# Recurrent layer with both directions in one tile of 1024 columns, and two-operand work taken off GpSimd

## The chip, the cores and the metric

The kernel runs on one core of a Trainium2 chip. The metric is the device time of one execution, in microseconds (us). Engines are named as the profile names them: PE (TensorE matmul), PEld (its weight load), DVE (VectorE), ACT (ScalarE), POOL (GpSimd) and SP (SyncE, which issues the large DMAs). L1404 is line 1404 of the kernel before.

## The reference

The model has two residual layers over 512 tokens of width 1024. Each is a mixer followed by a squared-ReLU MLP of width 4096. Layer 0 mixes with a state-space scan and attention; layer 1, which the change is about, with a recurrent block (RG-LRU). Cut to layer 1's mixer:

```
gate, xr = split(u @ rec_w_in)                 # (512, 1024) each
xc = causal/centred width-4 depthwise conv of xr over tokens
for direction in (forward, backward):
    r = sigmoid(blockdiag(xc, ra_w[direction]) + ra_b[direction])
    i = sigmoid(blockdiag(xc, ix_w[direction]) + ix_b[direction])
    log_a = -8 * r * softplus(-lam[direction])
    a = exp(log_a)
    b = sqrt(-expm1(2 * log_a)) * (i * xc)
    h = scan over tokens of h[t] = a[t] * h[t-1] + b[t]   # reversed for backward
    hs.append(h)
y = (hs[0] + hs[1]) * gelu(gate)
h_res = h_res + g1 * (y @ rec_w_out)
```

Then `u = rms_norm(h_res) * (1 + scale) + shift` feeds `h_res + g2 * (square(relu(u @ w1)) @ w2)`.

## The kernel before

Activations lie with features on the 128 partitions and tokens on the 512 columns; a tensor of width 1024 is eight such tiles (k = 0 to 7). Matmuls reach float32 precision with three float32r products: every weight tile and every activation is split into a rounded part `hi` and a rest `lo`, and PE adds hi*hi, hi*lo and lo*hi (L555 to L557 for dense layers, L528 to L530 for the small gate matrices). Splitting a weight tile of 1024 columns takes a cast (L508 on ACT, or L506 on POOL) and a subtraction (L509, on DVE or POOL).

The program is built once. A scheduler sets each engine's order of instructions ahead of time, from its own estimate of durations; on the chip each engine then works through its list in that order, and waits on semaphores. At the norm boundaries, and in the first quarter of the recurrent input projection, PE's order is that of the source (`manual`).

The parts that matter here, in order of time:

- **Norm boundaries** (`boundary`, L843 to L845): the last output tiles of a layer are summed and normalized in two halves of 256 tokens, while PE already works on the first half of the next layer. Per tile DVE runs L843 and L845, ACT L844. The first four weight tiles of the next layer are split meanwhile, and three times, ahead of MLP 0, ahead of the recurrent layer and ahead of MLP 1, their `lo` is computed on POOL (`lo_eng`).
- **Recurrent layer** (`rglru`). The input projection is done in four quarters of 512 output features: two of the recurrent branch, then two of the gate branch. `fetch` copies the first into `xp`, in token order (L1333); `conv` runs one POOL instruction (L1339) and three DVE instructions (L1341); `parts` splits the result into `xh` and `xl`. `gates` does, for each k and direction d, two block-diagonal matmuls, two tanh (L1374, into `tr` and `ti`), an exp (L1377, `a`), a tanh (L1378, `th`), the square of `a` (L1379, on POOL or DVE) and two fused DVE instructions (L1380, L1381). This is done for k = 0 to 3 (group 0) and k = 4 to 7 (group 1). After each group, `roots` takes eight square roots (L1397), a product (L1401, POOL or DVE), the scan forward (L1404) and backward (L1407), and their sum (L1408, POOL). `branch` applies gelu to the gate branch, `merge` multiplies (L1423), and L1468 and L1469 split the result for the output projection, which ends in the next norm boundary.

Of the buffers, `tr` has two tiles, `a` and `ti` eight each, all of 512 columns. `tok` and `perm` are views of the same 512 tokens: contiguous, and with a step of four elements.

## Time and profile before

| what | value |
| --- | --- |
| median of 3 runs (lowest to highest) | 1296.41 us (1295.36 to 1296.78) |
| the profiled execution's own time | 1295.61 us |
| its span, first to last instruction | 1293.8 us |
| PE busy in the span | 1188.2 us (92%) |
| DVE busy | 847.5 us (66%) |
| ACT busy | 525.8 us (41%) |
| POOL busy | 350.2 us (27%) |
| mean granted PE clock | 0.959 |

Busy time is a share of the whole span; the stages have different limits, so the rows further down are cut by stretches of time. Times in them count from the span's start. The recurrent layer fills about 735 to 910 us. The mean duration of a group holds waiting too, where an instruction has started and can't go on; the least duration of a form, in the answers that print least/median/longest, is the one without it.

### The profile page before, as it was taken

How to read it: one execution, taken by the hardware profiler on the slowest of the kernel's cores; microseconds unless marked ns; L12 is line 12 of the kernel's file. 1: busy time of each engine (PE TensorE's matmuls, PEld its weight loads, DVE VectorE, ACT ScalarE, POOL GpSimd, SP SyncE). 2: the span in 40 equal slices, each digit the busy share in tenths (PEclk: the TensorE clock that was granted, in tenths of full speed). 3: DMA queues.
4: the chain of work that ended last, by engine and by line, in shares of the span. 5: the costliest groups of instructions: out<-in, count | busy, mean ns of one | idle time of the engine just before them, and what ended most of it. 6: DMA issues, size and time to landing. Idle time of an engine off the chain costs nothing.

```text
span 1293.8 us, 17211 instructions
## 1 busy us (share of the span) xinstructions
PE 1188.2 (92%) x6552; PEld 1006.7 (78%) x6552; DVE 847.5 (66%) x1234; ACT 525.8 (41%) x954; POOL 350.2 (27%) x394
## 2 busy tenths in 40 slices
PE   2689999899999999999999997769899999999997
PEld 2578677777988888888889875558898888888887
DVE  7458999977878866487334799897655332435243
ACT  3157557454443421243322357563444311334130
POOL 9896886500200000000002477571300000000000
PEclk9989789999999999999999998789899999999998
DMA  9321311065448766576222321103233233332311
GB/s 326 126 62 57 91 30 33 20 201 171 163 130 273 248 211 193 167 250 193 96 96 81 115 82 35 63 17 114 66 98 98 98 98 98 98 98 94 97 38 66
DMA packets 83859, 151.77 MB, mean 117 GB/s; under 512 B 5696, under 2 KB 30272, under 8 KB 83776
## 3 DMA queue, kind: packets, MB, share of 16 engines
q1 hardware_dynamic: 75712, 137.04, 32.5%
q10 hardware_dynamic: 8064, 13.64, 3.3%
q8 instruction: 51, 0.84, 0.3%
q14 instruction: 32, 0.26, 0.1%
HBM read 148.55 MB, written 2.10 MB: 116 GB/s over the span
## 4 chain that ended last, share of the span: by engine, by line
PE 59%; DVE 22%; POOL 9%; issue 5%; DMA 3%; ACT 2%; DVEq 0%; POOLq 0%; ACTq 0%
PE ps L555 10%; PE ps L556 10%; PE ps L557 10%; PE px L555 7%; PE px L556 7%; PE px L557 7%; DVE actb L447 3%; DVE actb L845 2%; DMA wr<-ada_w 1%; DMA wr<-w 1%; DVE wl L509 1%; PE po L983 1%; DVE th L1404 1%; POOL tiny L77 1%; DVE acc L637 1%
## 5 line engine op out<-in xcount | busy, mean ns | idle before, releaser
L509 DVE TENSOR_TENSOR wl<-wr,wh 128x1024 fp32r<-128x1024 f32 (+2 forms) x163 | 198.8, 1222 | 278.7 <-ACT wh L508 272.3
L508 ACT CAST wh<-wr 128x1024 fp32r<-128x1024 f32 (+2 forms) x170 | 173.2, 1021 | 428.3 <-PE ps L556 190.5
L556 PE MATMUL ps<-actb,wh 128*128 128x512 f32 (+1 forms) x512 | 183.8, 359 | 0.0
L509 POOL TENSOR_TENSOR wl<-wr,wh 128x1024 fp32r<-128x1024 f32 (+1 forms) x15 | 34.6, 2310 | 461.3 <-ACT wh L508 458.5
L555 PE MATMUL ps<-acta,wh 128*128 128x512 f32 (+1 forms) x328 | 119.0, 363 | 2.1 <-ACT xp L1333 1.6
L557 PE MATMUL ps<-acta,wl 128*128 128x512 f32 (+1 forms) x328 | 117.9, 360 | 0.0
L555 PE MATMUL ps<-hid,wh 128*128 128x512 f32 x288 | 112.1, 389 | 0.0
L557 PE MATMUL ps<-hid,wl 128*128 128x512 f32 x288 | 112.0, 389 | 0.0
L556 PE MATMUL ps<-hid,wh 128*128 128x512 f32 x288 | 112.0, 389 | 0.0
L556 PEld LDWEIGHTS ps<-actb,wh 128*128 128x128 f32 x512 | 99.7, 195 | 13.5
L555 PE MATMUL px<-hid,wh 128*128 128x512 f32 (+1 forms) x288 | 98.9, 343 | 0.0
L557 PE MATMUL px<-hid,wl 128*128 128x512 f32 (+1 forms) x288 | 98.5, 342 | 0.0
L556 PE MATMUL px<-hid,wh 128*128 128x512 f32 (+1 forms) x288 | 98.5, 342 | 0.0
L556 PE MATMUL px<-actb,wh 128*128 128x512 f32 (+1 forms) x224 | 85.5, 382 | 0.0
L637 DVE SCALAR_TENSOR_TENSOR acc<-wr,cact,acc 128x1024 f32<-128x1024 f32 x49 | 62.8, 1281 | 17.5 <-DMA wr<-ada_w 16.8
L555 PEld LDWEIGHTS ps<-acta,wh 128*128 128x128 f32 x328 | 64.3, 196 | 12.1 <-ACT xp L1333 2.0
L557 PEld LDWEIGHTS ps<-acta,wl 128*128 128x128 f32 x328 | 64.0, 195 | 8.9
L555 PE MATMUL ps<-actc,wh 128*128 128x512 f32 (+1 forms) x184 | 65.8, 358 | 0.0
L557 PE MATMUL ps<-actc,wl 128*128 128x512 f32 (+1 forms) x184 | 65.3, 355 | 0.0
L555 PEld LDWEIGHTS ps<-hid,wh 128*128 128x128 f32 x288 | 54.1, 188 | 11.2
L557 PEld LDWEIGHTS ps<-hid,wl 128*128 128x128 f32 x288 | 54.1, 188 | 11.2
L556 PEld LDWEIGHTS ps<-hid,wh 128*128 128x128 f32 x288 | 54.1, 188 | 11.2
(493 smaller groups left out, 2877.8 us busy)
## 6 DMA issues: line engine op xcount, KB each, us to landing
wr<-w SPq DMA_DIRECT2D x128, 512.0 KB, 3.7
wr<-ada_w SPq DMA_DIRECT2D x56, 512.0 KB, 4.3
wr<-wout SPq DMA_DIRECT2D x16, 512.0 KB, 3.4
...
```

Source lines behind the costliest of these rows:

```text
L77: self.eng.tensor_scalar(t, a, s, None, op0=op0)
L447: self.scan = V.tensor_tensor_scan(vv, m4, vv, 0.0, op0=ALU.mult, op1=ALU.add)
L508: nc.scalar.copy(hi, src)
L509: (lo_eng or nc.vector).tensor_tensor(lo, src, hi.bitcast(F32), op=ALU.subtract)
L555: mm(out, wh, xh, start=first and a == a0 and lead(o), stop=False, skip_group_check=True)
L556: mm(out, wh, xl, start=False, stop=False, skip_group_check=True)
L557: mm(out, wl, xh, start=False, stop=last and a == a0 + kk - 1, skip_group_check=True)
L637: nc.vector.scalar_tensor_tensor(acc, raw, self.ca[:, k:k + 1], acc, op0=ALU.mult, op1=ALU.add)
L845: nc.vector.scalar_tensor_tensor(lo, t, sh[:, k:k + 1], hi.bitcast(F32), op0=ALU.add, op1=ALU.subtract)
L983: self.nc.tensor.matmul(po[h2 * 64:h2 * 64 + 64, t * 128:(t + 1) * 128], self.vp[:, kb, v], pts[:, kb * 128:(kb + 1) * 128], start=(kb == ...
L1404: V.tensor_tensor_scan(hs, a, ti, 0.0, op0=ALU.mult, op1=ALU.add)
```

## The change

It moves work between engines and joins the two directions. It leaves the matmuls, the number of weight tiles and all DMAs as they are.

- `gates` works on tiles of 1024 columns, d = 0 in the left half and d = 1 in the right. The matmuls, tanh and exp stay at 512 columns. The square of `a` becomes one ACT instruction of 1024 columns, and L1380 and L1381 become one DVE instruction each of 1024 columns. `tr` has two tiles of 1024, `a`, `ti` and `th` four each.
- `roots` takes one square root (ACT) and one product (DVE) of 1024 columns for each k; the scans stay at 512; the sum of the directions goes to DVE, into a new tile `hs`.
- `merge` writes the product contiguously into the gate tile and splits it at once; the separate loop with L1468 and L1469, which read with a step of four, is dropped.
- The `lo` of the gate matrices (`gwl`) and the `lo` of the first four weight tiles at the three boundaries go from POOL to DVE.
- Left on POOL from the first MLP on: two memsets for each `xp`, the first step of `conv`, the `hi` casts of the gate matrices, of `xh` for k under 4 and of eight weight tiles. All have one tensor operand.
- The pool `sp` no longer rounds its small tiles up to 512 bytes, which with a pad frees 4 KB a partition.

```diff
--- before.py
+++ after.py
@@ -56,7 +56,7 @@
 NCONST = 772
 
 LINE = 128
-ROUNDED = ("sp", "hyb", "att", "s5", "out", "mlp")
+ROUNDED = ("hyb", "att", "s5", "out", "mlp")
 
 XP = 640
 
@@ -144,6 +144,7 @@
         self.ap = self.pool(ctx, "ap")
         self.sp = self.pool(ctx, "sp")
         self.tl(self.pool(ctx, "edge", side="right"), "pad", [P, 120])
+        self.tl(self.sp, "pad", [P, 56])
         ct = self.cp.tile([P, NCOL], F32, tag="cols", name="cols_sb")
         nc.sync.dma_start(ct, cols)
         kt = self.cp.tile([P, NCONST], F32, tag="consts", name="consts_sb")
@@ -1276,12 +1277,12 @@
                 del hid[:]
                 for g in range(4):
                     if c == 0 and g == 0:
-                        self.hold, self.lo_eng = self.wdma, nc.gpsimd
+                        self.hold = self.wdma
                         with self.manual():
                             for hf, outs in enumerate(self.lin_half(w1, u, 0, 4, fresh=True)):
                                 for o in range(4):
                                     hidden(o, slice(hf * 256, hf * 256 + 256), outs[o])
-                                self.hold = self.lo_eng = None
+                                self.hold = None
                         continue
                     ps = self.lin(w1, u, c * 2048 + g * 512)
                     if side:
@@ -1346,7 +1347,7 @@
                     A.copy(hi, src)
                 else:
                     G.tensor_scalar(hi, src, 1.0, 0.0, op0=ALU.mult, op1=ALU.add)
-                (G if scalar is None else V).tensor_tensor(lo, src, hi.bitcast(F32), op=ALU.subtract)
+                V.tensor_tensor(lo, src, hi.bitcast(F32), op=ALU.subtract)
 
             def gate_split(k):
                 hi = self.tl(rp, "gwh", [P, 512], F32R, bufs=2)
@@ -1359,28 +1360,30 @@
                 split2(xh, xl, xc, k >= 4)
                 return xc, xh, xl
 
+            both = lambda t: t.rearrange("p (d n) -> p d n", d=2)
+
             def gates(k, xc, xh, xl):
 
-                out = []
                 wh, wl = gws[k] if k < 2 else gate_split(k)
+                tr = self.tl(rp, "tr", [P, 1024], bufs=2)
+                ti = self.tl(rp, "ti", [P, 1024], bufs=4)
                 for d in range(2):
                     j = d * 8 + k
-                    tr = self.tl(rp, "tr", [P, 512], bufs=2)
-                    ti = self.tl(rp, "ti", [P, 512], bufs=8)
                     for kind, o, b in ((0, tr, hra), (1, ti, hix)):
                         g = slice((d * 2 + kind) * P, (d * 2 + kind + 1) * P)
                         ps = self.psum("pn" if (d, kind) == (0, 1) else "px")
                         self.mm3(ps, wh[:, g], wl[:, g], xh, xl, True, True)
-                        sig = A.activation(o, ps, AF.Tanh, bias=b[:, j:j + 1], scale=0.5)
-                    a = self.tl(rp, "a", [P, 512], bufs=8)
-                    th = self.tl(rp, f"th{d}", [P, 512], bufs=8 - 4 * d)
-                    A.activation(a, tr, AF.Exp, bias=nsp4[:, j:j + 1], scale=nsp4[:, j:j + 1])
-                    last = A.activation(th, tr, AF.Tanh, bias=sp4[:, j:j + 1], scale=sp4[:, j:j + 1])
-                    (V if k < 4 and d == 1 else G).tensor_tensor(tr, a, a, op=ALU.mult)
-                    V.scalar_tensor_tensor(th, tr, 1.0, th, op0=ALU.add, op1=ALU.mult)
-                    V.scalar_tensor_tensor(ti, ti, 1.0, xc, op0=ALU.add, op1=ALU.mult)
-                    out.append((a, th, ti))
-                return out, (sig, last)
+                        sig = A.activation(both(o)[:, d], ps, AF.Tanh, bias=b[:, j:j + 1], scale=0.5)
+                a = self.tl(rp, "a", [P, 1024], bufs=4)
+                th = self.tl(rp, "th", [P, 1024], bufs=4)
+                for d in range(2):
+                    j = d * 8 + k
+                    A.activation(both(a)[:, d], both(tr)[:, d], AF.Exp, bias=nsp4[:, j:j + 1], scale=nsp4[:, j:j + 1])
+                    A.activation(both(th)[:, d], both(tr)[:, d], AF.Tanh, bias=sp4[:, j:j + 1], scale=sp4[:, j:j + 1])
+                last = A.activation(tr, a, AF.Square)
+                V.scalar_tensor_tensor(th, tr, 1.0, th, op0=ALU.add, op1=ALU.mult)
+                V.scalar_tensor_tensor(both(ti), both(ti), 1.0, xc.unsqueeze(1).to_broadcast([P, 2, 512]), op0=ALU.add, op1=ALU.mult)
+                return (a, th, ti), (sig, last)
 
             def behind(ins):
                 st = ExitStack()
@@ -1391,21 +1394,16 @@
             def roots(g, gt, after):
 
                 with behind(after):
-                    for o in range(4):
-                        for d in range(2):
-                            th = gt[o][d][1]
-                            last = (A.activation(th, th, AF.Sqrt, scale=0.25),)
-                for o in range(4):
-                    for d in range(2):
-                        a, th, ti = gt[o][d]
-                        (V if g == 0 and d == 1 else G).tensor_tensor(ti, ti, th, op=ALU.mult)
-                        if d == 0:
-                            hs = th
-                            V.tensor_tensor_scan(hs, a, ti, 0.0, op0=ALU.mult, op1=ALU.add)
-                            hfs[g * 4 + o] = hs
-                        else:
-                            V.tensor_tensor_scan(ti[:, ::-1], a[:, ::-1], ti[:, ::-1], 0.0, op0=ALU.mult, op1=ALU.add)
-                            G.tensor_tensor(hs, hs, ti, op=ALU.add)
+                    for a, th, ti in gt:
+                        last = (A.activation(th, th, AF.Sqrt, scale=0.25),)
+                for o, (a, th, ti) in enumerate(gt):
+                    V.tensor_tensor(ti, ti, th, op=ALU.mult)
+                    hs = self.tl(rp, "hs", [P, 512], bufs=8)
+                    a, ti = both(a), both(ti)
+                    V.tensor_tensor_scan(hs, a[:, 0], ti[:, 0], 0.0, op0=ALU.mult, op1=ALU.add)
+                    V.tensor_tensor_scan(ti[:, 1, ::-1], a[:, 1, ::-1], ti[:, 1, ::-1], 0.0, op0=ALU.mult, op1=ALU.add)
+                    V.tensor_tensor(hs, hs, ti[:, 1], op=ALU.add)
+                    hfs[g * 4 + o] = hs
                 return last
 
             def branch(ps, after, gg=()):
@@ -1418,17 +1416,24 @@
                 return gg, last
 
             def merge(g, gg):
+
                 for o in range(4):
-                    hs = hfs[g * 4 + o]
-                    V.tensor_tensor(perm(hs), tok(gg[o]), perm(hs), op=ALU.mult)
-
+                    if o % 2 == 0:
+                        hi2, lo2 = (both(self.tl(rp, t, [P, 1024], F32R, bufs=4)) for t in ("a", "ti"))
+                    hi, lo = hi2[:, o % 2], lo2[:, o % 2]
+                    V.tensor_tensor(tok(gg[o]), tok(gg[o]), perm(hfs[g * 4 + o]), op=ALU.mult)
+                    A.copy(hi, gg[o])
+                    V.tensor_tensor(lo, gg[o], hi.bitcast(F32), op=ALU.subtract)
+                    ys.append((hi, lo))
+
+            ys = []
             xps = [None] * 4
-            self.hi_eng, self.lo_eng = None, G
+            self.hi_eng = None
             with self.manual():
                 for hf, outs in enumerate(self.lin_half(win, u, 1024, 4, fresh=True)):
                     for o in range(4):
                         xps[o] = fetch(o, outs[o], hf, xps[o])
-            self.hi_eng, self.lo_eng = G, None
+            self.hi_eng = G
             last = ()
             cvs = [None] * 4
             for g in range(2):
@@ -1461,13 +1466,6 @@
             merge(0, gg)
             gg, last = branch(ps, last)
             merge(1, gg)
-            ys = []
-            for o in range(8):
-                hi = self.tl(rp, "a", [P, 512], F32R, bufs=8)
-                lo = self.tl(rp, "ti", [P, 512], F32R, bufs=8)
-                A.copy(tok(hi), perm(hfs[o]))
-                V.tensor_tensor(tok(lo), perm(hfs[o]), tok(hi).bitcast(F32), op=ALU.subtract)
-                ys.append((hi, lo))
             self.rotate(["ps", "ps", "ps", "ps", "px", "px", "px"])
 
             def upd(k, sl, ps):
```

The order of the instructions moves at these places. The first is DVE's list at the norm boundary ahead of the recurrent layer, from the second half of the first 256 tokens to the statistics of the other half. Before (L845 writes the `lo` half of the new activations, L1272 updates the residual, L730 and L733 are the statistics):

```order
L845 SCALAR_TENSOR_TENSOR actb_6783<-nt_6784,mod_4813,acta_6782 128x256
L845 SCALAR_TENSOR_TENSOR actb_6789<-nt_6784,mod_4813,acta_6788 128x256
L1272 SCALAR_TENSOR_TENSOR h_3732<-px_6690,mod_4422,h_3732 128x256
L1272 SCALAR_TENSOR_TENSOR h_3736<-px_6690,mod_4422,h_3736 128x256
L845 SCALAR_TENSOR_TENSOR actb_6794<-nt_6795,mod_4813,acta_6793 128x256
L845 SCALAR_TENSOR_TENSOR actb_6800<-nt_6795,mod_4813,acta_6799 128x256
L730 TENSOR_SCALAR nr1x_6921<-pn_6914 128x2
```

Of the change, the same stretch (its line numbers are one higher from L147 on):

```order
L1273 SCALAR_TENSOR_TENSOR h_3733<-px_6691,mod_4423,h_3733 128x256
L1273 SCALAR_TENSOR_TENSOR h_3737<-px_6691,mod_4423,h_3737 128x256
L510 TENSOR_TENSOR wl_7008<-wr_7006,wh_7007 128x1024
L846 SCALAR_TENSOR_TENSOR actb_6784<-nt_6785,mod_4814,acta_6783 128x256
L846 SCALAR_TENSOR_TENSOR actb_6790<-nt_6785,mod_4814,acta_6789 128x256
L846 SCALAR_TENSOR_TENSOR actb_6795<-nt_6796,mod_4814,acta_6794 128x256
L1350 TENSOR_TENSOR gwl_7169<-gw_6862,gwh_7168 128x512
L846 SCALAR_TENSOR_TENSOR actb_6801<-nt_6796,mod_4814,acta_6800 128x256
L1350 TENSOR_TENSOR gwl_7182<-gw_6864,gwh_7181 128x512
L731 TENSOR_SCALAR nr1x_6922<-pn_6915 128x2
```

Four `wl` (three of them earlier in the list) and two `gwl` now stand in DVE's own list between the norm's instructions, where POOL ran them beside it.

The second place is DVE's list at the end of group 1, from the last fused instruction to the first `lo` of the output projection's activations (scans are printed as SCALAR_TENSOR_TENSOR). Before:

```order
L1380 SCALAR_TENSOR_TENSOR th_1611_7860<-tr_7847,th_1611_7860 128x512
L1404 SCALAR_TENSOR_TENSOR th_1546_7603<-a_7602,ti_7591 128x512
L1407 SCALAR_TENSOR_TENSOR ti_7610<-a_7621,ti_7610 128x512
L1404 SCALAR_TENSOR_TENSOR th_1567_7686<-a_7685,ti_7674 128x512
L1423 TENSOR_TENSOR th_1456_7227<-xh_7866,th_1456_7227 128x4x128
L1423 TENSOR_TENSOR th_1475_7306<-xl_7867,th_1475_7306 128x4x128
L1407 SCALAR_TENSOR_TENSOR ti_7693<-a_7704,ti_7693 128x512
L1423 TENSOR_TENSOR th_1496_7389<-xh_7868,th_1496_7389 128x4x128
L1423 TENSOR_TENSOR th_1514_7463<-xl_7869,th_1514_7463 128x4x128
L1404 SCALAR_TENSOR_TENSOR th_1588_7769<-a_7768,ti_7757 128x512
L509 TENSOR_TENSOR wl_8084<-wr_8082,wh_8083 128x1024
L1469 TENSOR_TENSOR ti_8047<-th_1456_7227,a_8046 128x512
```

Of the change (L1400 is the product of 1024 columns, L1403 and L1404 the scans, L1405 the sum, L1424 the merge, L1426 the `lo`):

```order
L1384 SCALAR_TENSOR_TENSOR th_7799<-tr_7776,th_7799 128x1024
L1400 TENSOR_TENSOR ti_7560<-ti_7560,th_7582 128x1024
L1403 SCALAR_TENSOR_TENSOR hs_7944<-a_7581,ti_7560 128x512
L1404 SCALAR_TENSOR_TENSOR ti_7560<-a_7581,ti_7560 128x512
L1400 TENSOR_TENSOR ti_7777<-ti_7777,th_7799 128x1024
L1424 TENSOR_TENSOR xh_7807<-xh_7807,hs_7484 128x512
L1405 TENSOR_TENSOR hs_7944<-hs_7944,ti_7560 128x512
L1424 TENSOR_TENSOR xl_7810<-xl_7810,hs_7499 128x512
L510 TENSOR_TENSOR wl_8013<-wr_8011,wh_8012 128x1024
L510 TENSOR_TENSOR wl_8043<-wr_8041,wh_8042 128x1024
L1404 SCALAR_TENSOR_TENSOR ti_7777<-a_7798,ti_7777 128x512
L1426 TENSOR_TENSOR ti_7968<-xh_7807,a_7967 128x512
```

Rows of the same kind are left out of both: from the last fused instruction to the first `lo` DVE's list of the change holds four products, eight scans, four merges, two sums and two `wl`. The products and sums are new on DVE here.

The third place is PE's list for the gates of k = 5 to 7 (L529 to L531 of the change are the gate matmuls, L556 to L558 the dense ones). Before, at most twelve gate matmuls stood in a row. Of the change, the end of a run of 30:

```order
L529 MATMUL px_7778<-xh_7673,gwh_7772 128x512
L529 MATMUL px_7788<-xh_7673,gwh_7772 128x512
L529 MATMUL px_7793<-xh_7673,gwh_7772 128x512
L529 MATMUL pn_7783<-xh_7673,gwh_7772 128x512
L530 MATMUL px_7778<-xl_7674,gwh_7772 128x512
L531 MATMUL px_7778<-xh_7673,gwl_7773 128x512
L531 MATMUL px_7793<-xh_7673,gwl_7773 128x512
L556 MATMUL ps_7815<-acta_6761,wh_7820 128x512
```

The dense matmuls of the third quarter stand ahead of that run and the 96 of the last quarter behind it, where before the two kinds alternated and 69 dense ones were left behind the last gate. SP's list of DMAs is the same in both.

## Rows read from the trace of the kernel before

**Rows 1.** The page's busy times: us, share of the span, instructions.
```profile
PE 1188.2 (92%) x6552; PEld 1006.7 (78%) x6552; DVE 847.5 (66%) x1234; ACT 525.8 (41%) x954; POOL 350.2 (27%) x394
```

**Rows 2.** Busy time by engine: first, second stretch, tail, output projection; a ten-us one.
```profile
735.00:788.20 53.20, 48.48 (x221) 38.80 (x220) 48.32 (x47) 28.95 (x42) 39.53 (x37) 0.98 0.30 96
788.20:844.80 56.60, 42.29 (x143) 31.63 (x142) 50.27 (x48) 35.84 (x51) 34.63 (x21) 0.75 0.11 38
844.80:870.20 25.40, 13.91 (x63) 11.19 (x61) 24.22 (x15) 17.72 (x25) 23.94 (x11) 0.81 0.03 7
870.20:910.50 40.30, 39.04 (x223) 34.41 (x223) 28.67 (x36) 13.78 (x21) 6.25 (x1) 0.95 0.31 101
...
840.00:850.00 10.00, 10.00 (x46) 8.29 (x45) 6.39 (x7) 9.54 (x15) 6.72 (x5) 1.00 0.01 2
```

**Rows 3.** What PE waited for, 735 to 890: us in total, times, longest.
```profile
PE ps L556 <- DVE ti L1469: 12.8, 2, 11.5
PE px L528 <- ACT tr L1374: 9.8, 4, 5.4
PE px L529 <- DVE xl L1349: 4.1, 3, 2.3
PE ps L555 <- ACT xp L1333: 1.6, 1, 1.6
```

**Rows 4.** DVE's forms by line: duration in ns least/median/longest, first and last start.
```profile
L1381 DVE SCALAR_TENSOR_TENSOR ti<-ti,xc x12: 677/900/1751, 756.4 to 834.0; 128x512 f32<-128x512 f32 x12
L1341 DVE SCALAR_TENSOR_TENSOR xc<-xp,cols_sb,xc x18: 739/1092/1527, 739.4 to 791.0; 128x512 f32<-128x512 f32 x18
L1404 DVE TENSOR_TENSOR_SCAN th<-a,ti x8: 1191/2264/2303, 798.5 to 871.0; 128x512 f32<-128x512 f32 x8
L1469 DVE TENSOR_TENSOR ti<-th,a x8: 1046/1072/2041, 868.1 to 888.0; 128x512 fp32r<-128x512 f32 x8
L1423 DVE TENSOR_TENSOR th<-xp,th x4: 1081/1098/1100, 873.2 to 883.9; 128x512 f32<-128x512 f32 x4
L509 DVE TENSOR_TENSOR wl<-wr,wh x20: 1193/1224/2276, 731.7 to 896.3; 128x1024 fp32r<-128x1024 f32 x20
```

**Rows 5.** POOL and DVE side by side: start, us, engine, line.
```profile
756.43 1.10 DVE L1381 SCALAR_TENSOR_TENSOR ti<-ti,xc 128x512 f32<-128x512 f32 x1
...
756.96 1.05 POOL L1348 TENSOR_SCALAR xh<-xc 128x512 fp32r<-128x512 f32 x1
757.97 1.29 POOL L1349 TENSOR_TENSOR gwl<-gw,gwh 128x512 fp32r<-128x512 f32 x1
...
758.04 1.77 DVE L1349 TENSOR_TENSOR xl<-xc,xh 128x512 fp32r<-128x512 f32 x1 [0.52 <-POOL xh L1348]
```

**Rows 6.** POOL's groups, 335 to 935: busy us, mean ns, idle before.
```profile
L509 POOL TENSOR_TENSOR wl<-wr,wh 128x1024 fp32r<-128x1024 f32 x12 | 29.2, 2434 | 461.3 <-ACT wh L508 458.5 <-issue 2.8
L1401 POOL TENSOR_TENSOR ti<-ti,th 128x512 f32<-128x512 f32 x12 | 23.9, 2019 | 2.0 <-ACT th L1397 2.0
```

**Rows 7.** ACT's groups, 735 to 890: busy us, mean ns, idle before.
```profile
L1377 ACT ACTIVATE a<-tr,rgc 128x512 f32<-128x512 f32 x16 | 13.0, 815 | 0.2
L508 ACT CAST wh<-wr 128x1024 fp32r<-128x1024 f32 x11 | 11.5, 1043 | 3.3 <-issue 2.7 <-PE ps L556 0.6
L1374 ACT ACTIVATE tr<-px,rgc 128x512 f32<-128x512 f32 x16 | 10.9, 687 | 27.4 <-PE px L530 12.0 <-DVE th L1380 11.7 <-PE pn L530 3.4
```

**Rows 8.** Norm boundaries: PE's waits, DVE behind POOL, and a stretch at half clock.
```profile
PE pn L802 <- DVE nr1y L735: 2.3, 1, 2.3
...
PE pn L795 <- DVE nacc L781: 3.8, 1, 3.8
...
916.12 5.26 DVE L845 SCALAR_TENSOR_TENSOR actb<-nt,mod,acta 128x256 fp32r<-128x256 f32 x3
...
929.00:936.00 7.00, 7.00 (x35) 7.00 (x35) 0.94 (x6) 0.20 (x1) 0.00 (x0) 0.51 0.18 63
```

**Rows 9.** POOL's longest single instruction of the recurrent layer.
```profile
877.58 6.25 POOL L1408 TENSOR_TENSOR th<-th,ti 128x512 f32<-128x512 f32 x1 [8.27 <-DVE ti L1407]
```

## The prediction

> **What bounds the kernel now.** I began with the page's busy times [rows 1]: PE is busy 92% of the span, so time is to be had only where PE waits or runs slowly. The table by stretches shows where that is [rows 2]: in the recurrent layer. From 788.2 to 844.8 us PE is busy 42.3 of 56.6 us, at a mean granted clock of 0.75, for 143 matmuls. At full rate (2.4 GHz) 46 matmuls of 512 columns take 10 us, 0.217 us each [rows 2], so these are 31 us of work. The list of PE's waits names what it lacked [rows 3]: DVE's `lo` tiles (L1469, L1349), and ACT's tanh, which waits for `tr`, which DVE's L1380 has to free. ACT is not full (35.8 us of that stretch), DVE nearly is (50.3) [rows 2].
>
> Much of DVE's time there is not work. The scan takes 1.19 us at least and 2.26 at the median, the fused L1381 0.68 and 0.90, with 1.75 at the longest [rows 4]. The side-by-side rows show the reason: DVE's subtraction that starts 0.07 us behind a two-operand POOL instruction takes 1.77 us instead of 0.68, so it stood until POOL's 1.29 us were over; behind a one-operand one L1381 took 1.10, a loss of 0.42 [rows 5]. POOL is busy 39.5, 34.6 and 23.9 us in the first three stretches [rows 2], and its products mean 2.02 us [rows 6]: the two engines block each other.
>
> The Trainium skill, "SBUF — State Buffer", section "Who interferes with whom", says that a DVE instruction with two SBUF inputs contends with any GpSimd instruction that reads SBUF, and that the later one blocks until the other ends. By that rule the change's line between one operand and two is none, and the time would be the 1305 us of the first rival below; the trace agrees that one-operand instructions block at all, with 0.42 us where POOL ran for 1.05 [rows 5].
>
> **The change, part by part.** Each price is a least duration [rows 4], since it counts work without blocking: 0.68 us for two inputs of 512 columns, 0.74 for a conv step, 1.2 for 1024 columns or a scan, 1.06 to 1.09 for a read with a step of four.
>
> DVE's work from 735 to 890 now: 17 weight `lo` x 1.2, 24 conv steps x 0.74, 52 instructions of 512 x 0.68, 16 scans x 1.2, 8 + 8 strided ones x 1.07 make 110 us. The change makes 32 fused ones of 512 into 16 of 1024 (21.8 to 19.2), the four products of 512 into eight of 1024 (2.7 to 9.6), drops four squares (2.7), adds six gate `lo` and eight sums (9.5), and takes the step out of eight `lo` (8.4 to 5.4): some 118 us. So DVE gets 8 us more work, and should get rid of the blocking behind two-operand instructions. POOL keeps 28 instructions of about 1.05 us [rows 5], 29 us instead of the 98 us of the first three stretches. Twelve weight `lo`, 29.2 us on POOL [rows 6], become 12 x 1.2 = 14.5 us on DVE, at the boundaries.
>
> *First stretch, 735 to 788.2 (group 0).* PE's waits on L1349 and on `xp`, up to 5.7 us [rows 3], are what can go; DVE's added and dropped work nearly cancel here. I take a **gain of 4**; the ends are 0 and 6.
>
> *Second stretch, 56.6 us: roots of group 0, gates of group 1.* DVE's list holds twelve instructions of 1024 (14.4), eight scans (9.6), eight sums and copies (5.4) and about eleven splits and conv steps (8.5): 38 us, plus a few us behind POOL. ACT has its 35.8 us now [rows 2] and four squares of 1024 columns; none stands in the trace, the nearest row is the cast of 1024 at 1.04 us [rows 7], so 40 us. Eight roots of 512 become four of 1024, counted even. PE needs 31. No engine needs more than 40, and the chain tanh, exp, square, fused product still runs through three engines; `tr`, with two tiles of 1024, now lets gates run a whole k ahead. I take 43 us, since DVE stands at most a k's work (some 3 us) in front of ACT: a **gain of 14**. The ends: 40, a gain of 17; or ACT's 40 with all the 20.8 us that it waits in this stretch today, a loss of 4.
>
> *Tail, 844.8 to 870.2.* PE's longest wait, 11.5 us, ends with the first L1469 [rows 3]. By its list DVE now runs four products, eight scans, four merges, two sums and two weight `lo` before that `lo`: 4.8 + 9.6 + 4.3 + 1.4 + 2.4 = 22.5 us, plus about 2 us until the first root of 1024 columns is out. That is about what the stretch took with blocking (25.4 less the `lo` itself): the moved products eat what the missing POOL gives. **Gain 0**, ends -3 and 3. PE meanwhile has 96 dense matmuls, 20.8 us.
>
> *Output projection, 870.2 to 910.5.* PE is busy 39.0 of 40.3 us at clock 0.95 [rows 2]: PE bounds it. The second wait on L1469, 12.8 less 11.5 us [rows 3], goes, and some of the slow clock: **gain 2**, ends 0 and 3.
>
> *The three boundaries.* PE waits 2.3 us ahead of the recurrent layer and 3.8 ahead of MLP 1, then runs 7 us at clock 0.51 (1.2 GHz for 2.4) [rows 8], 35 matmuls of half work lost, about 3.4 us; the clock fell behind the wait. DVE's L845, three of which took 5.26 us, stood behind POOL [rows 8]. Against that, DVE takes over four weight `lo`, 4.8 us, at each. The sums nearly balance, but at the first of these places the statistics no longer stand behind gate `lo` of POOL. **Gain 4** for all; the ends are 9 (waits and slow clock gone) and a loss of 7 (half of the 14.5 us uncovered).
>
> `sp`'s new packing I cost at nothing: no row prices it, and its tiles are written by instructions that lie beside PE's work. The memsets, table loads, DMAs and SP's order stay.
>
> The sum is 4 + 14 + 0 + 2 + 4 = **24 us**. From the profiled execution's 1295.61 us, of which 1293.8 are span, that leaves 1271.6; this execution lies 0.8 under the median of the runs, so I predict **1272 us**.
>
> **The rivals.**
>
> *One-operand POOL instructions block as much.* If each of the 28 costs DVE its 1.05 us, 29 us of blocking stay. What is there today is about 32 us: DVE's busy time to 890 (the first three stretches, 122.8 us, and some 19 of the 28.7 us behind them [rows 2]) less its 110 of work. Then DVE saves 3 and gets 8 more in the layer, and some 4 more at the boundaries: **1305 us**, slower than before. It decides at about 0.7 us per POOL instruction. (The rule of the Trainium skill's SBUF page, above, would give this.) For it: the one-operand instruction in the rows did cost 0.42 us. Against: 0.42 is well under 1.05, and a POOL list of 28 rarely meets DVE at the start of an instruction. Chance 10%, of which 2 in the band of no change.
>
> *POOL is starved instead.* With DVE's list dense in two-input instructions, POOL waits: L1408 took 6.25 us where DVE streamed [rows 9]. POOL still begins each conv and casts eight weight tiles. If each of eight k loses PE 1.5 us: 12 us, **1284 us**. Against: those steps are issued a k ahead. Chance 13%.
>
> *PE loses its filler.* PE's list now has 30 gate matmuls in a row ahead of the last quarter. They wait for ACT, which needs about 7 us per k (four tanh, four exp and tanh, a square [rows 7]) where PE needs 12 x 0.217 = 2.6. If PE's clock falls to half there, as it does today at mean 0.75 [rows 2], and half of the 96 dense matmuls behind the gates run at half clock, the tail waits for PE instead: about 10 us, **1282 us**. Chance 15%.
>
> *All of it.* The upper ends, 6 + 17 + 3 + 3 + 9 = 38 us: DVE's blocking was all that held PE. **1258 us**. Chance 12%.
>
> **How the numbers follow.** The forecast has 50%, between about 1264 and 1279. The range that takes in the three faster cases reaches from 1258 to 1287 and leaves out the slower rival and the outermost part of the ends. Faster than before by over 0.2% (2.6 us, about what a measurement of this kernel can tell from none): the forecast and the three cases, 90%. Within 0.2%: 3%. Slower: 7%.
>
> **What would show it.** Right: DVE's scans at 1.2 us at the median; DVE busier with fewer us per instruction; the second stretch near 43 us and the first `lo` of the output projection some 18 us earlier against the start of the layer; PE's mean clock there over 0.85; the wait of 2.3 us gone. Wrong: fused instructions of 1024 that take 1.6 us or more beside POOL's one-operand ones; PE waiting for weight tiles (`wh` of L506) or for `xh`; PE at half clock after 850 us; `wl` on DVE delaying L845 at the boundaries, so that the waits of 3.8 us grow.

## The result, and the profile after

The changed kernel takes **1261.7 us** (median of 4 runs, 1260.99 to 1262.24), the kernel before beside it 1296.6. The ratio is 0.973, with a 95% interval of 0.9713 to 0.9747: a gain of 33 to 37 us. The forecast was 1272, with a range of 1258 to 1287. The direction and the range held; the gain was under-sized by some 10 us.

The page's busy times of the changed kernel, to be read beside [rows 1]:

```profile
PE 1174.1 (93%) x6552; PEld 997.9 (79%) x6552; DVE 820.2 (65%) x1246; ACT 527.5 (42%) x954; POOL 244.9 (19%) x342
```

DVE runs twelve instructions more than before and is busy 27 us less, though by the forecast's prices it took over some 22 us of work. What went is time it had spent standing.

The table by stretches of the changed kernel, cut at the same events as [rows 2]: the first stretch, from the same matmul on, to the first roots; the second, to the last L1384; the tail, to PE's first matmul on a `lo` of the output projection; the output projection, to the first matmul of the next boundary's statistics; and the first 5.9 us of that projection alone. Columns: the window and its length, then busy us (instructions) of PE, PEld, DVE, ACT and POOL, the granted clock, DMA share, GB/s.

```profile
729.50:777.10 47.60, 47.60 (x228) 40.13 (x227) 42.85 (x44) 33.55 (x49) 26.60 (x29) 1.00 0.32 101
777.10:818.10 41.00, 32.26 (x117) 24.70 (x117) 38.19 (x42) 35.91 (x48) 3.31 (x3) 0.83 0.17 58
818.10:842.10 24.00, 18.70 (x82) 14.87 (x81) 22.85 (x23) 16.73 (x22) 0.00 (x0) 0.98 0.12 38
842.10:881.10 39.00, 39.00 (x221) 34.60 (x221) 23.84 (x35) 11.65 (x21) 0.00 (x0) 0.93 0.27 86
...
842.10:848.00 5.90, 5.90 (x14) 4.64 (x15) 5.90 (x8) 0.62 (x1) 0.00 (x0) 0.51 0.33 116
```

The first stretch takes 47.6 us (53.2 before), the second 41.0 (56.6), the tail 24.0 (25.4), the output projection 39.0 (40.3). POOL has nothing to do in the tail now. In the second stretch DVE (38.2 of 41.0) and ACT (35.9) are close to full and PE is not, so the bound has passed from blocking to work. The last row shows what a wait still costs: behind its wait of 4.4 us PE runs at a granted clock of 0.51, 1.2 GHz for 2.4.

PE's waits of the changed kernel, first from 730 to 890 us, then at the norm boundaries (us in total, times, longest). `nacc` and `nr1y` are steps of the norm's statistics. The rows answer to [rows 3] and [rows 8]:

```profile
PE ps L557 <- DVE ti L1426: 4.4, 1, 4.4
PE pn L529 <- ACT ti L1376: 4.2, 1, 4.2
PE px L530 <- DVE xl L1350: 2.8, 1, 2.8
PE px L529 <- ACT ti L1376: 1.5, 1, 1.5
...
PE pn L796 <- DVE nacc L782: 1.8, 1, 1.8
PE pn L803 <- DVE nr1y L736: 0.8, 1, 0.8
```

The wait for the first `lo` fell from 11.5 to 4.4 us. The 9.8 us of waits for tanh into `tr` are down to 0.2; waits for tanh into `ti`, 5.7 us, took part of their place. At the boundaries 5.9 us behind nacc (two waits, 2.1 and 3.8) became one of 1.8, and 2.3 became 0.8.

DVE's forms by line in the changed kernel (ns, least/median/longest), to be read against [rows 4]: the scans, the fused instruction of 1024 columns, conv and the weight `lo`:

```profile
L1403 DVE TENSOR_TENSOR_SCAN hs<-a,ti x8: 1211/1215/1228, 788.0 to 839.1; 128x512 f32<-128x512 f32 x8
L1385 DVE SCALAR_TENSOR_TENSOR ti<-ti,xc x6: 1212/1214/1214, 753.2 to 811.1; 128x1024 f32<-128x1024 f32 x6
L1342 DVE SCALAR_TENSOR_TENSOR xc<-xp,cols_sb,xc x18: 737/867/1528, 734.0 to 775.0; 128x512 f32<-128x512 f32 x18
L510 DVE TENSOR_TENSOR wl<-wr,wh x28: 1196/1222/1629, 698.4 to 894.0; 128x1024 fp32r<-128x1024 f32 x28
```

The forecast's price list holds to a few hundredths of a microsecond: the scan's median went from 2.26 us to 1.215. Of the forms shown, only the conv steps, which stand beside POOL's casts, still have a median well above their least.

### The profile page after: what moved, and what is told of

Its sections match the earlier page's. It is cut to its first block, busy times and chain, and to the rows that moved or that the text cites. A ratio compares the mean times of both kernels' runs of the same rounds, so it can differ in the third digit from the quotient of the medians.

```text
span 1260.4 us, 17174 instructions
## 1 busy us (share of the span) xinstructions
PE 1174.1 (93%) x6552; PEld 997.9 (79%) x6552; DVE 820.2 (65%) x1246; ACT 527.5 (42%) x954; POOL 244.9 (19%) x342
## 3 DMA queue, kind: packets, MB, share of 16 engines
q1 hardware_dynamic: 75712, 137.04, 33.4%
## 4 chain that ended last, share of the span: by engine, by line
PE 71%; DVE 15%; POOL 8%; issue 3%; ACT 3%; DMA 0%; DVEq 0%; ACTq 0%; POOLq 0%
PE ps L557 12%; PE ps L558 12%; PE ps L556 12%; PE px L556 8%; PE px L557 8%; PE px L558 8%; DVE actb L448 2%; DVE wl L510 2%; PE po L984 1%; POOL tiny L77 1%; DVE actb L443 1%; DVE s5m L442 1%; DVE actb L441 1%; DVE nb L966 1%; DVE ti L1404 1%
## 5 line engine op out<-in xcount | busy, mean ns | idle before, releaser
L510 DVE TENSOR_TENSOR wl<-wr,wh 128x1024 fp32r<-128x1024 f32 (+2 forms) x175 | 211.3, 1209 | 288.5 <-ACT wh L509 277.9
L557 PE MATMUL ps<-actb,wh 128*128 128x512 f32 (+1 forms) x512 | 181.1, 354 | 0.1
L556 PE MATMUL ps<-acta,wh 128*128 128x512 f32 (+1 forms) x328 | 116.5, 356 | 0.0
L558 PE MATMUL ps<-acta,wl 128*128 128x512 f32 (+1 forms) x328 | 115.9, 354 | 0.0
L556 PE MATMUL ps<-hid,wh 128*128 128x512 f32 x288 | 112.1, 389 | 0.0
L558 PE MATMUL ps<-hid,wl 128*128 128x512 f32 x288 | 112.0, 389 | 0.0
L556 PE MATMUL px<-hid,wh 128*128 128x512 f32 (+1 forms) x288 | 98.9, 343 | 0.0
L558 PE MATMUL px<-hid,wl 128*128 128x512 f32 (+1 forms) x288 | 98.4, 342 | 0.0
L556 PEld LDWEIGHTS ps<-acta,wh 128*128 128x128 f32 x328 | 62.7, 191 | 8.5
L558 PEld LDWEIGHTS ps<-acta,wl 128*128 128x128 f32 x328 | 62.6, 191 | 8.4
L556 PE MATMUL ps<-actc,wh 128*128 128x512 f32 (+1 forms) x184 | 65.1, 354 | 0.0
L558 PE MATMUL ps<-actc,wl 128*128 128x512 f32 (+1 forms) x184 | 64.8, 352 | 0.0
L556 PEld LDWEIGHTS ps<-hid,wh 128*128 128x128 f32 x288 | 54.1, 188 | 11.3
L558 PEld LDWEIGHTS ps<-hid,wl 128*128 128x128 f32 x288 | 54.1, 188 | 11.2
```

What stands on the lines that cost most here:

```text
L510: (lo_eng or nc.vector).tensor_tensor(lo, src, hi.bitcast(F32), op=ALU.subtract)
L556: mm(out, wh, xh, start=first and a == a0 and lead(o), stop=False, skip_group_check=True)
L557: mm(out, wh, xl, start=False, stop=False, skip_group_check=True)
L558: mm(out, wl, xh, start=False, stop=last and a == a0 + kk - 1, skip_group_check=True)
```

## The experiments

Twelve runs. Times are medians; the ratio is to the kernel before in the same session, with its interval. In the sessions the kernel before had medians of 1296.0 to 1297.0 us, so a difference between runs of two sessions is uncertain by about 1 us more.

| run | what it is | us | ratio |
| --- | --- | --- | --- |
| e1 | before, boundary `lo` on DVE | 1286.6 | 0.9918 (0.9903 to 0.9932) |
| e2 | before, layer's two-operand work off POOL | 1281.4 | 0.9875 (0.9861 to 0.9890) |
| e3 | e1 and e2 together | 1270.1 | 0.9788 (0.9771 to 0.9804) |
| e4 | changed, layer's two-operand work back on POOL, but for the squares | 1281.5 | 0.9877 (0.9863 to 0.9892) |
| e5 | changed, POOL's casts with two operands | 1275.0 | 0.9836 (0.9820 to 0.9852) |
| e6 | changed, old merge | 1262.0 | 0.9735 (0.9720 to 0.9749) |
| e7 | changed, gelu and merge of group 0 first | 1255.5 | 0.9685 (0.9671 to 0.9700) |
| e8 | before, new packing of `sp` | 1296.9 | 1.0000 (0.9991 to 1.0009) |
| e9 | e3 with four `tr` of 512 columns | 1262.4 | 0.9741 (0.9725 to 0.9758) |
| e10 | e7, backward scan into `th` | 1261.0 | 0.9724 (0.9704 to 0.9744) |
| e11 | before, four `tr` of 512 columns | 1296.3 | 0.9992 (0.9982 to 1.0001) |
| e12 | e7, all `xh` casts on POOL | 1259.5 | 0.9712 (0.9698 to 0.9726) |

### e1: the boundaries alone

```diff
-                        self.hold, self.lo_eng = self.wdma, nc.gpsimd
+                        self.hold = self.wdma
...
-            self.hi_eng, self.lo_eng = None, G
+            self.hi_eng = None
```

> The kernel before, with nothing changed but the engine of the twelve `lo` of weight tiles at the three norm boundaries: DVE for POOL. Theory (POOL's two-operand instructions held DVE up, at the boundaries too, and that part of the gain is about 9 us): 1288 us, 1286 to 1290, the waits of 2.1, 2.3 and 3.8 us for nacc and nr1y smaller, and L845 at its least duration. Rival (DVE only trades 29.2 us on POOL for 14.5 us of its own): 1294 to 1300.

Measured: 1286.6 us, 10.4 less than before (9 to 13 by the interval). The boundary ahead of MLP 1 in this run, in the timeline of DVE (start, us, engine, line, and in brackets the idle time before it), and then PE's waits of the boundaries:

```profile
906.47 1.23 DVE L509 TENSOR_TENSOR wl<-wr,wh 128x1024 fp32r<-128x1024 f32 x1 [2.63 <-ACT wh L508]
...
911.38 1.22 DVE L509 TENSOR_TENSOR wl<-wr,wh 128x1024 fp32r<-128x1024 f32 x1
912.51 1.66 DVE L845 SCALAR_TENSOR_TENSOR actb<-nt,mod,acta 128x256 fp32r<-128x256 f32 x4
```

```profile
PE pn L795 <- DVE nacc L781: 1.8, 1, 1.8
PE pn L802 <- DVE nr1y L735: 1.7, 1, 1.7
```

Four L845 take 1.66 us where three took 5.26 [rows 8], and a `wl` takes 1.23 us on DVE where POOL took 2.43 [rows 6]. The first of the four stands in time in which DVE was idle; the other three (from 911.38, 914.88 and 919.16 us) stand in its list, 1.22 us each, 3.7 in all. In the kernel before, the four on POOL cost DVE 5.9 us at this boundary, counted above the least durations: 4.0 on the three L845 of [rows 8], 0.6 on a step of the statistics, and 1.3 on these two L845, which take 0.87 us without blocking:

```profile
925.96 2.17 DVE L845 SCALAR_TENSOR_TENSOR actb<-nt,mod,acta 128x256 fp32r<-128x256 f32 x2
```

The theory holds: the `wl` cost DVE less in its own list than they had cost it from POOL. Two details differ. PE's waits at the boundaries fell by 4.7 us (8.2 to 3.5), so they are not the whole of the gain. And ahead of the recurrent layer four L845 still take 4.42 us, beside gate `lo` that this run leaves on POOL.

### e2, e3 and e4: the layer's two-operand work, with and without the joining

e2 changes the kernel before as follows, and nothing else; e3 has this and e1's edit.

```diff
-                (G if scalar is None else V).tensor_tensor(lo, src, hi.bitcast(F32), op=ALU.subtract)
+                V.tensor_tensor(lo, src, hi.bitcast(F32), op=ALU.subtract)
...
-                    last = A.activation(th, tr, AF.Tanh, bias=sp4[:, j:j + 1], scale=sp4[:, j:j + 1])
-                    (V if k < 4 and d == 1 else G).tensor_tensor(tr, a, a, op=ALU.mult)
+                    A.activation(th, tr, AF.Tanh, bias=sp4[:, j:j + 1], scale=sp4[:, j:j + 1])
+                    last = A.activation(tr, a, AF.Square)
...
-                        (V if g == 0 and d == 1 else G).tensor_tensor(ti, ti, th, op=ALU.mult)
+                        V.tensor_tensor(ti, ti, th, op=ALU.mult)
...
-                            G.tensor_tensor(hs, hs, ti, op=ALU.add)
+                            V.tensor_tensor(hs, hs, ti, op=ALU.add)
```

> The kernel before, at 512 columns and with its old merge, the boundaries' `lo` left on POOL; only the two-operand work of the recurrent layer leaves POOL: the gate `lo`, the products and the sums go to DVE, the squares to ACT (16 of 512 columns). DVE gets about 15 us more of least durations (26 moved instructions less four squares, 0.68 each). Theory (blocking): most of the 24 us that the layer and its output projection gave, less the 7 us that 512 columns cost DVE where they are not hidden: 1276 us, 1272 to 1280. Rival (the joining of the directions, with its deeper tr and fewer instructions, is what gave the gain): 1290 us or more, since DVE was nearly full.

> Both edits of the two runs ahead of this one together: the kernel before, without two-operand work on POOL, but not joined, and with the old merge. Theory (blocking, and the two parts simply add): 1267 us, 1262 to 1271, so that joining and merge are worth about 5 us of the 34.7. Rival (joining): 1282 us or more.

Measured: 1281.4 and 1270.1 us, gains of 15.7 and 26.9. The theory holds in direction, though e2 lies 1.4 us above its upper end: DVE got some 15 us more work (the estimate of the expectation), and the kernel still became faster. The two gains add (10.4 + 15.7 = 26.1). What is left to the changed kernel is 8.4 us, more than the 5 expected.

e4 goes the other way, in the changed kernel:

```diff
-                V.tensor_tensor(lo, src, hi.bitcast(F32), op=ALU.subtract)
+                (G if scalar is None else V).tensor_tensor(lo, src, hi.bitcast(F32), op=ALU.subtract)
...
-                    V.tensor_tensor(ti, ti, th, op=ALU.mult)
+                    (V if g == 0 and o % 2 else G).tensor_tensor(ti, ti, th, op=ALU.mult)
...
-                    V.tensor_tensor(hs, hs, ti[:, 1], op=ALU.add)
+                    G.tensor_tensor(hs, hs, ti[:, 1], op=ALU.add)
```

> The changed kernel, joined, with its merge and its boundaries, but the gate `lo` (8), the products of 1024 columns (6 of 8, as many as before by columns) and the sums (8) back on POOL. Theory (blocking): scans near 2.2 us at the median again, and 1278 us, 1273 to 1285. Rival (joining gave the gain): 1266 us or less.

Measured: 1281.5 us, so 22 instructions on POOL cost 19.8 us. DVE's forms by line (ns, least/median/longest), and one of PE's waits:

```profile
L1403 DVE TENSOR_TENSOR_SCAN hs<-a,ti x8: 1192/1213/3395, 793.5 to 855.2; 128x512 f32<-128x512 f32 x8
...
L1384 DVE SCALAR_TENSOR_TENSOR th<-tr,th x8: 1207/1425/3357, 755.8 to 828.7; 128x1024 f32<-128x1024 f32 x8
```

```profile
PE px L529 <- ACT tr L1376: 11.4, 2, 6.5
```

The time lies in the theory's range. The detail does not: the scans' median stays at 1.21 us, since only three of these eight scans lose time. In the trace from 690 to 935 us five DVE instructions lose about 2.2 us each, behind POOL's products of 1024 columns, and some fifteen about 1.1, behind its other two-operand instructions.

### e5: one operand against two

```diff
-                G.tensor_scalar(xc, xp[:, 0:512], cw[:, 4 * k:4 * k + 1], self.col["cb"][:, k:k + 1], op0=ALU.mult, op1=ALU.add)
+                G.tensor_tensor(xc, xp[:, 0:512], xp[:, 0:512], op=ALU.add)
...
-                    G.tensor_scalar(hi, src, 1.0, 0.0, op0=ALU.mult, op1=ALU.add)
+                    G.tensor_tensor(hi, src, src, op=ALU.add)
...
+        if eng is nc.gpsimd and eng is self.hi_eng:
+            nc.gpsimd.tensor_tensor(hi, src, src, op=ALU.add)
```

> The changed kernel, in which GpSimd's own casts and first conv steps in the recurrent layer become two-operand additions of the same size (a tile added to itself); nothing moves to another engine. It leaves out precision and the conv's first weight and bias: `hi` is rounded from twice the value, and `lo` takes the rest, so the work is of the same kinds and sizes. Theory (it is the second operand that holds DVE up): 1268 us, 1264 to 1274; conv steps and splits on DVE beside POOL lose some 0.6 to 0.9 us each instead of 0.3. Rival (any GpSimd instruction that reads SBUF holds DVE up alike, and the change gained by the smaller number alone): 1262 us, within 2 us of the changed kernel.

Measured: 1275.0 us, 13.2 slower than the changed kernel with the same number of POOL instructions. The rival falls. The timelines of POOL and DVE, four pairs side by side (start, us, engine, line); first the changed kernel, a cast of 512 columns and one of 1024, each with the conv step that started behind it:

```profile
743.22 1.05 POOL L1349 TENSOR_SCALAR xh<-xc 128x512 fp32r<-128x512 f32 x1
743.72 1.09 DVE L1342 SCALAR_TENSOR_TENSOR xc<-xp,cols_sb,xc 128x512 f32<-128x512 f32 x1
...
748.15 1.24 POOL L507 TENSOR_SCALAR wh<-wr 128x1024 fp32r<-128x1024 f32 x1
748.39 1.53 DVE L1342 SCALAR_TENSOR_TENSOR h<-xp,cols_sb,h 128x512 f32<-128x512 f32 x1
```

and the same two pairs in e5:

```profile
748.72 1.48 POOL L1351 TENSOR_TENSOR xh<-xc 128x512 fp32r<-128x512 f32 x1 [0.63 <-DVE xc L1344]
749.22 1.52 DVE L1344 SCALAR_TENSOR_TENSOR h<-xp,cols_sb,h 128x512 f32<-128x512 f32 x1
...
750.23 2.26 POOL L507 TENSOR_TENSOR wh<-wr 128x1024 fp32r<-128x1024 f32 x1
750.67 2.38 DVE L1344 SCALAR_TENSOR_TENSOR xc<-xp,cols_sb,xc 128x512 f32<-128x512 f32 x1
```

The conv step's least is 0.74 us. It loses 0.35 behind a one-operand cast of 512 columns and 0.79 behind one of 1024; 0.78 and 1.64 behind the two-operand ones. So both kinds block, and the price goes with the number of elements that POOL reads: two operands of 512 cost what one of 1024 does. Each loss is about a quarter of a microsecond under the least duration of POOL's own form (ns, least/median/longest), 0.62 and 1.05 us here, 1.03 and 1.89 for the two-operand forms in e5:

```profile
L1349 POOL TENSOR_SCALAR xh<-xc x3: 620/1049/1052, 740.8 to 751.5; 128x512 fp32r<-128x512 f32 x3
L507 POOL TENSOR_SCALAR wh<-wr x8: 1047/1143/1405, 725.1 to 763.6; 128x1024 fp32r<-128x1024 f32 x8
```

The medians are longer, as POOL in its turn stands behind DVE.

My theory, that the second operand as such holds DVE up, is thus too coarse, and its upper end of 1274 was 1 us too low. With 20 instructions of 512 columns and 8 of 1024, the changed kernel's POOL list would cost DVE 20 x 0.35 + 8 x 0.79 = 13.3 us if each instruction met one of DVE's, and e5's twice that. The traces come close: what DVE's instructions from 690 to 935 us take above the least of their line and form adds up to 12.1 us in the changed kernel, 23.8 in e5, and 54.4 in the kernel before. The 11.7 us between the first two are most of e5's 13.2; POOL's own results also come later in e5, and these runs do not part the two.

The Trainium skill, "SBUF — State Buffer", section "Who interferes with whom", says that a DVE instruction with two SBUF inputs contends with any GpSimd instruction that reads SBUF; the trace agrees, with the 0.35 and 0.79 us behind casts of one operand. It also says that the later one blocks until the other ends; the trace agrees, as in all four pairs the conv step ends 0.53 to 0.56 us behind POOL's instruction, less than the 0.74 that it needs by itself, so it stood until shortly before that end. A POOL instruction that reads less ends sooner. So the prediction's 1305 us came not from the rule but from the 1.05 us put into it.

### e6, e8, e9 and e11: what the rest is

e6 puts the old merge into the changed kernel, e8 only the new packing into the kernel before.

```diff
-                    V.tensor_tensor(tok(gg[o]), tok(gg[o]), perm(hfs[g * 4 + o]), op=ALU.mult)
-                    A.copy(hi, gg[o])
-                    V.tensor_tensor(lo, gg[o], hi.bitcast(F32), op=ALU.subtract)
+                    hs = hfs[g * 4 + o]
+                    V.tensor_tensor(perm(hs), tok(gg[o]), perm(hs), op=ALU.mult)
...
+                A.copy(tok(hi), perm(hfs[o]))
+                V.tensor_tensor(tok(lo), perm(hfs[o]), tok(hi).bitcast(F32), op=ALU.subtract)
```

> The changed kernel with the old merge: product in token order, then the separate loop with a cast (ACT) and a `lo` (DVE) that read with a step of four. Theory (of the 8.4 us between the run without two-operand POOL work and the changed kernel, the 5.8 us at the start of the output projection are the merge's): 1267 us, 1265 to 1269, PE waiting again on the cast of the output projection. Rival (all 8.4 us are the joining's): 1262 us.

```diff
-ROUNDED = ("sp", "hyb", "att", "s5", "out", "mlp")
+ROUNDED = ("hyb", "att", "s5", "out", "mlp")
...
+        self.tl(self.sp, "pad", [P, 56])
```

> The kernel before with nothing but the new packing of the sp pool and its pad. Forecast's cost of nothing: 1297 us, within 1.5. Rival (some of the gain comes from new addresses): 1294 or less.

Measured: 1262.0 us for e6, the changed kernel's time, and 1296.9 for e8, that of the kernel before. My reading, that the merge was worth 5.8 us, fell: with the old merge PE's wait for the first `lo` of the projection is 3.4 us in e6, with the new one 4.4. That the waits in e3's output projection came from a late start of its merge is not shown. The packing costs and gives nothing by itself.

e9 is e3 with the depth of `tr` that the joining brings, and without the joining:

```diff
-                    tr = self.tl(rp, "tr", [P, 512], bufs=2)
+                    tr = self.tl(rp, "tr", [P, 512], bufs=4)
```

> The kernel before without any two-operand work on POOL from the first MLP on, not joined, old merge, and now with four tr buffers of 512 columns for two (the bytes of two of 1024; the new packing of sp makes the room). The old merge in the changed kernel cost nothing, so the 8.4 us between the run without two-operand work and the changed kernel are the joining's. Theory (they come from tr: without the joining ACT's tanh waits 7.7 us in all for the tr that L1380 frees, in the changed kernel it doesn't): 1263 us, 1261 to 1266, that wait gone. Rival (fewer and larger instructions, with less fixed cost on DVE and ACT): 1270 us, within 2 us of the run without the deeper tr.

Measured: 1262.4 us, 7.7 less than e3 by the medians (6 by the ratios). ACT's wait for `tr`, 735 to 830 us, in e3, and the same in e9, 735 to 820:

```profile
ACT tr L1374 <- DVE th L1380: 7.7, 4, 3.2
```

```profile
ACT tr L1375 <- DVE th L1381: 3.5, 2, 2.3
```

The theory holds: e9 and the changed kernel lie 0.7 us apart, within both intervals, so the deeper `tr` is 6 to 8 us, and the larger instructions and the merge have no gain of their own that these runs can tell. The wait was halved and not, as expected, removed.

e11 is e9's depth in the kernel before, with POOL's work left as it was.

> The kernel before with nothing but four tr buffers for two (and the packing that makes their room); POOL keeps all its two-operand work. Theory (PE's 9.8 us of waits on ACT's tanh came from tr's two buffers, whatever held DVE up, so the depth gives its 7.7 us here too): 1289 us, 1287 to 1291. Rival (with DVE held up by POOL the stretch is full, and the deeper tr only moves the wait): 1294 to 1298 us.

Measured: 1296.3 us, no change. The rival holds; PE's waits, 730 to 900 us:

```profile
PE px L529 <- ACT tr L1375: 13.4, 2, 8.1
PE px L530 <- DVE xl L1350: 9.5, 4, 6.9
PE ps L557 <- DVE ti L1470: 7.2, 2, 6.6
```

PE's wait for tanh grew from 9.8 us [rows 3] to 13.4, and the ones for `xl` from 7.0 (4.1 of [rows 3] and the row below, of the kernel before) to 9.5, while the one for the `lo` of the output projection fell from 12.8 to 7.2. A deeper buffer in front of a blocked DVE only moves the waits.

```profile
PE pn L529 <- DVE xl L1349: 2.9, 1, 2.9
```

### e7, e10 and e12: a faster version, and two that were not

e7 changes the order at the end of the layer. The merge of group 0, whose scans are long done, no longer stands behind the roots of group 1; it writes into the buffers of `tr`, `gwh` and `gwl`.

```diff
-            last = roots(1, gt, last)
             gg, last = branch(raw, last, raw)
             merge(0, gg)
+            last = roots(1, gt, last)
...
+                    if g == 0:
+                        if o % 2 == 0:
+                            hi2 = both(self.tl(rp, "tr", [P, 1024], F32R, bufs=2))
+                        lo2 = {o % 2: self.tl(rp, ("gwh", "gwl")[o // 2], [P, 512], F32R, bufs=2)}
```

> The changed kernel with another order at its end: the gelu of the first gate quarter and the merge of group 0 stand ahead of the roots of group 1, and that merge writes into the buffers of tr, gwh and gwl, which are free by then. It costs one more table load on ACT (1.3 us or so). Theory (the tail is DVE's list of 22 us in which the first `lo` stands last, so its order, not its length, sets PE's wait of 4.4 us and the half clock behind it): 1256 us, 1253 to 1259, the wait gone. Rival (ACT's extra load and the later roots of group 1 make PE wait in the middle of the output projection instead): 1262 to 1266 us.

Measured: **1255.5 us**, 6.2 less than the changed kernel, and the fastest of all runs here. The table by stretches, over the changed kernel's tail, and PE's wait for a `lo`:

```profile
819.30:842.10 22.80, 22.80 (x103) 18.86 (x102) 22.37 (x23) 16.61 (x22) 0.00 (x0) 1.00 0.07 24
```

```profile
PE ps L557 <- DVE ti L1430: 2.3, 1, 2.3
```

The theory holds: DVE has as much to do as in the changed kernel (22.4 of these 22.8 us), but PE is busy throughout, at full clock, and starts the projection on group 0. A smaller wait, 2.3 us, comes back in the middle of the projection, so something of the rival is in it too.

e10 and e12 build on e7. e10 lets the backward scan write into `th`, so that `ti` comes free earlier; e12 casts `xh` on POOL for all k.

```diff
-                    V.tensor_tensor_scan(ti[:, 1, ::-1], a[:, 1, ::-1], ti[:, 1, ::-1], 0.0, op0=ALU.mult, op1=ALU.add)
+                    V.tensor_tensor_scan(th[:, 1, ::-1], a[:, 1, ::-1], ti[:, 1, ::-1], 0.0, op0=ALU.mult, op1=ALU.add)
```

> The version with the gelu of the first quarter ahead of the roots of group 1 (1255.5 us), in which the backward scan writes into the right half of th, so that ti is free for group 1 after the scans and not only after the sum of the directions. Theory (PE's wait of 4.25 us at 798 us, with half clock behind it, is ACT's tanh waiting for a ti that the sum L1405 frees): 1252 us, 1249 to 1254. Rival (ACT and DVE are full there, or the th held longer stops the tanh into th instead): 1255 us or more.

```diff
-                split2(xh, xl, xc, k >= 4)
+                split2(xh, xl, xc)
```

> The version with the gelu of the first quarter ahead of the roots of group 1 (1255.5 us), with the four casts of xh for k = 4 to 7 on POOL instead of ACT, one operand each. Theory (ACT, busy 36.8 of 42.3 us in the second stretch, is what PE waits for there, POOL is idle, and a one-operand instruction costs DVE 0.3 us at most): 1253 us, 1251 to 1255. Rival (POOL's cast takes 1.05 us and more for ACT's 0.6, and DVE's xl waits for it): 1255 to 1260 us.

Measured: 1261.0 and 1259.5 us, both slower than e7 and in the range of their rivals. In e10 ACT still waits 2.0 us for `ti`, now behind the backward scan and not the sum (2.1 in e7), and a wait for `th`, in the chain's next place, came on top (ACT's waits, 735 to 820 us). Order moved in the tail as well, so the cause of the 5.5 us stays open:

```profile
ACT th L1382 <- DVE hs L1405: 2.5, 1, 2.5
```

In e12 PE waited for POOL's cast, 1.2 of the 4.0 us; the rest is not traced. The 0.3 us a cast of its theory was too low, by the 0.35 of e5. PE's wait, then POOL's two casts ahead of it in the timeline, and DVE's instructions beside the first:

```profile
PE px L529 <- POOL xh L1349: 1.2, 1, 1.2
```

```profile
803.30 4.68 POOL L1349 TENSOR_SCALAR gwh<-gw 128x512 fp32r<-128x512 f32 x1 [20.95 <-PE pn L530]
807.95 0.61 POOL L1349 TENSOR_SCALAR xh<-h 128x512 fp32r<-128x512 f32 x1
```

```profile
802.82 1.27 DVE L1405 TENSOR_TENSOR hs<-hs,ti 128x512 f32<-128x512 f32 x2
804.03 2.34 DVE L1384 SCALAR_TENSOR_TENSOR th<-tr,th 128x1024 f32<-128x1024 f32 x2
806.30 1.21 DVE L1385 SCALAR_TENSOR_TENSOR ti<-ti,xc 128x1024 f32<-128x1024 f32 x1
```

A cast of 512 columns, 0.61 us undisturbed, took 4.68 while DVE ran its two-input instructions back to back, and ended 0.47 us after the last of them. The `xh` that PE waited for stood behind it. This is the forecast's "POOL is starved", in a place where PE waits for the result.

## Why the prediction was right, and where it was off

By the trace the span fell by 33.4 us (1293.8 to 1260.4) for the 24 of the sum. The terms:

| term | forecast | measured | from |
| --- | --- | --- | --- |
| first stretch | 4 | 5.6 | 53.2 less 47.6 |
| second stretch | 14 | 15.6 | 56.6 less 41.0 |
| tail | 0 | 1.4 | 25.4 less 24.0 |
| output projection | 2 | 1.3 | 40.3 less 39.0 |
| boundaries | 4 | 9.5 | 5.5 ahead of the layer (735 to 729.5), 2.3 from the output projection to the end of PE's wait ahead of MLP 1 (18.1 less 15.8), 1.7 behind it |

- **The boundaries** are the term that was mis-sized, by 5.5 of the 9.4 us. The step that failed is "Against that, DVE takes over four weight `lo`, 4.8 us, at each. The sums nearly balance". I set DVE's new work against PE's waits and slow clock, as if all of it stood on the path, and gave the blocking in DVE's list no price. e1 shows them apart: 10.4 us of gain from this edit alone. Ahead of MLP 1 the four `wl` cost DVE's list 3.7 us (one lies in a gap), and from POOL they had cost it 5.9. The upper end of 9 was the better number, but not for its reason, "waits and slow clock gone": 2.6 of the 8.2 us of waits are left, and behind the wait ahead of MLP 1 PE still runs for seven us at a clock of 0.76 (897.3 to 904.3 us), where it was 0.51 [rows 8].
- **The second stretch** was right in size (43 us forecast, 41.0 measured) and right in its bound: no engine is busy over 38.2 us. Taking the two-operand work off POOL gives the most of it: cut at the same events, the stretch takes 44.1 us in e2 and 43.3 in e3. The deeper `tr`, "lets gates run a whole k ahead", stood in this term as half a sentence and without a price. It is worth 6 to 8 us once POOL no longer blocks (e9 against e3) and nothing while it does (e11), and most of it falls elsewhere. The first and second stretch of e3, then of e9:

```profile
730.20:782.30 52.10, 52.08 (x247) 43.48 (x246) 44.76 (x53) 34.31 (x52) 28.02 (x30) 1.00 0.31 98
782.30:825.60 43.30, 32.05 (x119) 23.26 (x118) 37.89 (x53) 36.41 (x56) 5.24 (x3) 0.88 0.14 49
```

```profile
729.80:777.80 48.00, 48.00 (x230) 40.45 (x229) 44.32 (x51) 33.90 (x53) 26.50 (x29) 1.00 0.31 100
777.80:819.10 41.30, 31.61 (x113) 23.30 (x113) 39.28 (x55) 36.34 (x56) 3.28 (x3) 0.79 0.17 57
```

- **The first stretch and the tail** gained 1.6 and 1.4 us more than forecast, within their ends. The first stretch's reason, that PE's waits there can go, does not carry its number: in e3 PE is busy throughout it and it still takes 52.1 us. The deeper `tr` takes off 4.1 more, as the first roots start with 17 matmuls fewer ahead of them. That the forecast of 4 came near was in part luck. The tail's reading, that moved products eat what the missing POOL gives, was right in its sum: DVE is busy 22.9 us there, 22.5 forecast. That the order inside this list, and not its length, set PE's wait was not seen; e7 shows it.
- **The parts that were costed evenly or at nothing**: the packing (e8) and the larger roots (7.9 us of ACT for 8.8) held. The contiguous merge was counted at 3 us of DVE and gave nothing to be measured (e6).
- **One-operand blocking** (the rival on the slower side) fell by its price. It assumed 1.05 us for each instruction, POOL's duration in the row. But 0.43 of that POOL itself stood behind DVE, as its form takes 0.62 us at least. The row of 0.42 that I set against it was the better guide, with 0.35 measured for 512 columns and 0.79 for 1024: 13.3 us for 28, or 0.48 each, under the 0.7 at which this rival decides.
- **PE loses its filler** came in part: the second stretch ran at a clock of 0.83 and the first 5.9 us of the projection at 0.51, but the waits behind it were 4.2 and 4.4 us, not ten. **POOL is starved** cost PE nothing directly in the changed kernel (no wait of PE names POOL); e12 shows where it would.

Of the signs named ahead of the run, these came out: scans at 1.2 us, the second stretch at 41.0 (near 43), PE's first matmul on a `lo` of the projection earlier by 22.6 us against the start of the layer (forecast 18). Three did not: the wait of 2.3 us is down to 0.8 and not gone, PE's mean clock of the second stretch, 0.83, missed the 0.85 narrowly, and DVE is not busier, with 820.2 us for 847.5. One of the signs of being wrong showed once: of the eight L1384 one took 2.06 us beside POOL's casts.

Not settled: whether the joining's larger instructions are worth anything once the order of e7 is used, and how e10 and e12 would stand in e7's exact order, since an edit lets the scheduler move its neighbours.
